# The sums of the FFN input's blocks, made by pairs of token tiles as they leave the norm

## The chip, the cores and the metric

The kernel runs on one core of one Trainium2 chip. The metric is the time of one execution in device microseconds (us); the median of three runs is shown. A core has five engines that each work through a list of instructions in its own order: TensorE (PE, with its weight loads as PEld), VectorE (DVE), ScalarE (ACT), GpSimd (POOL) and SyncE (SP). SP issues nearly all DMAs here. An instruction that waits for a semaphore holds back all that stand behind it on its engine.

## The reference

One inference step of one layer: attention and a diagonal state-space branch, merged and projected by `w_out`, and then a gated feed-forward part (FFN), for 1024 prompt tokens and 64 sample tokens in float32. The part that matters here:

```python
x = x + _rmsnorm(merged @ W['w_out'], W['norm_mix_post'])
f = _rmsnorm(x, W['norm_ffn_pre'])                 # (1088, 1024)
f = (jax.nn.silu(f @ W['w_ffn_gate']) * (f @ W['w_ffn_up'])) @ W['w_ffn_down']   # D_FF = 2816
x = x + _rmsnorm(f, W['norm_ffn_post'])
```

## The kernel before, in words

**Numbers in two halves.** A float32 operand is split into a high part (ACT rounds it to fp32r, line 125) and a low part (DVE takes the difference, line 126). A product then takes three matmuls, high by high, high by low and low by high. `split` is this pair of an ACT and a DVE instruction.

**The mix stage** (`mix_out`). The tokens go through in nine tiles, 8 (the 64 sample tokens), then 0 to 7 of 128 tokens. For a tile, PE makes the product with `w_out` in two banks of 512 columns (lines 137 to 139, 48 matmuls), then `post` normalizes it and adds the residual (ACT line 982, POOL line 148, DVE line 986, POOL line 987), SP writes it to DRAM (`x2`), and `pre` normalizes it once more (ACT line 1010, DVE line 1012), transposes it on PE (line 1016, two groups of four 128 by 128 transposes, each group in one bank of PSUM, tag `tr`, of which there are two) and splits each group into `H`. `H` holds the FFN's input by features: [128, 8 groups of features, high and low, 1088 tokens]. Three tiles' banks let PE run ahead of the norms.

**The FFN's first half** (`ffn_in`). `D_FF` is cut into 11 parts of 256, p = 0 to 10, and each part has a step for the gate weights and one for the up weights. The input is cut into 2 by 2 blocks, features 0 to 511 and 512 to 1023 (r) by tokens 0 to 511 and 512 to 1023 (c). p = 0 (`ffn_first`) is a plain product: for c = 0 gate and up, then for c = 1. Each of p = 1 to 10 uses Winograd's form of Strassen's scheme: seven block products in place of eight, with sums of input blocks (`t1` to `t4`, high and low) on one side and sums of weight blocks (`s1` to `s4`, POOL line 1120, then split) on the other. With X11, X12, X21, X22 for the input's blocks (feature half, token half), the sums are t1 = X12 - X11, t2 = X22 - t1, t3 = X22 - X12 and t4 = X21 - t2. `wino_mm` (line 1184) issues twelve matmuls of 512 columns per block product. The 64 sample tokens go by `decode_rows` (line 1160), whose operand `HD` is a copy of H's last 64 columns (ACT line 1192).

**The token sums** (`wino_tokens`, lines 1056 to 1090). After `ffn_first`, DVE and POOL add the halves in `H` again to whole numbers, make the sums, and split them: t2, t3 and t4 into tiles `T2`, `T3`, `T4`, and t1 over block (0, 1) of `H`, which only p = 0 needs in its plain form. They use buffers (`c`, `s`, `st`) that the weight sums use too.

**The down weights' sums** (`down_sums`). For each p, POOL makes the sums of the down weights' blocks and SP writes them to DRAM (`td`); the second half of the FFN, after p = 10, reads them.

**What sets the order.** The code is recorded in the order of the loops, and a scheduler then orders each engine's instructions by its own model of when each would be ready. The order is fixed when the program is built, for each engine and for SP's queue of DMAs. So a buffer's number of copies (`bufs`) decides who waits for whom, and the scheduler's order decides who stands behind the one that waits.

Of the kernel before, what the change touches and what calls it, by code (L numbers as in the profile page):

```python
# [8 lines left out]
F32 = mybir.dt.float32  # L9
F32R = mybir.dt.float32r  # L10
BF = mybir.dt.bfloat16
AF = mybir.ActivationFunctionType
# [3 lines left out]

D = 1024
SEQ = 1024
# [3 lines left out]
HD = 64  # L22
SBW = 512
FF = 2816
EPS = 1e-6
T = 8
NCH = SEQ // T + 1 + DEC // T
S0 = SEQ // T + 1
CH = ((0, 364), (364, 362), (726, 362))
# [39 lines left out]
class Net:  # L69
# [5 lines left out]
    def consts(self):  # L75
# [22 lines left out]
        nc.vector.memset(self.mhalf, -0.5)  # L98
        self.H = K.tile([128, 8, 2, TOK], F32R, name="H")

# [200 lines left out]
    def ssm_tables(self, P, S):  # L301
# [79 lines left out]
        lp, lpc, fp = pair(lam), pair(lam, True), pair(f)  # L381
        wt = S.tile([128, 2, 16, T, 16], F32, name="wt")
        tm = [S.tile([128, 2, 16, 16], F32, name=f"tm{i}", tag=f"tm{i}") for i in range(2)]
        self.cmul(V, wt[:, :, :, 0], braw, braw[:, ::-1], *bc(fp, 16), tm)
        for n in range(1, T):
            x = wt[:, :, :, n - 1]
# [614 lines left out]
            nc.vector.scalar_tensor_tensor(x[:, s], fg[:, s], rs, xres[:, s], op0=OP.mult, op1=OP.add)  # L1001
            nc.sync.dma_start(out[:, s], x[:, s])

    def pre(self, P, x, gb, hi, lo):

        nc = self.nc
        r = x.shape[0]
        ss = P.tile([128, 4], F32, "ss", "ss")[:r]
        xn = P.tile([128, D], F32, "xn", "xn")[:r]
        nc.scalar.activation(xn, x, AF.Square, scale=1 / 32.0, accum_out=ss[:, 0:1])  # L1010
        rs = self.rstd(P.pool, ss[:, 0:1])
        nc.vector.scalar_tensor_tensor(xn, x, rs, gb[:r], op0=OP.mult, op1=OP.mult)
        for k0 in (0, 4):
            ps = self.ps.tile([128, 512], F32, name="tr", tag="tr")
            for k in range(4):
                nc.tensor.transpose(ps[:, k * 128:k * 128 + r], xn[:, (k0 + k) * 128:(k0 + k + 1) * 128], self.ident[:r, :r])
            self.split(hi[:, k0:k0 + 4], lo[:, k0:k0 + 4], ps.rearrange("p (k t) -> p k t", k=4)[:, :, :r])

    def rows(self, dst, prompt, sample, t):
        self.nc.sync.dma_start(dst, prompt[t * 128:(t + 1) * 128] if t < 8 else sample)  # L1020
# [9 lines left out]
    def mix_out(self, P, U):  # L1030
        nc = self.nc
        self.x2 = self.dram.tile([TOK, D], F32, name="x2")
        gb, gp = self.bcast(P, "norm_mix_post"), self.bcast(P, "norm_ffn_pre")
        for t in (8, 0, 1, 2, 3, 4, 5, 6, 7):
            r, c0 = 128 if t < 8 else DEC, t * 128
            xr = P.tile([128, D], F32, "xr", "xr")[:r]
            self.rows(xr, self.I["x_prompt"][0], self.I["x_sample"][0], t)
            x = P.tile([128, D], F32, "xo", "xo")[:r]
            f = []
            for n in range(2):  # L1040
                s = slice(n * 512, (n + 1) * 512)
                ps = self.ps.tile([128, 512], F32, name="pj", tag="pj")
                if t < 8:
                    self.mm3(ps, [self.hk(k, c0, 128) + (h[:, s], l[:, s]) for k, (h, l) in enumerate(U)])
                    f.append(ps)
                else:
                    self.mm2(ps, [(self.HS[:, k], h[:, s], l[:, s]) for k, (h, l) in enumerate(U)])
                    y = P.tile([128, D], F32, "xn", "xn")[:r, :512]
                    self.low_rows(y, ps, x[:, s])
                    f.append(y)  # L1050
            self.post(P, f, gb, xr, x, x)
            nc.sync.dma_start(self.x2[c0:c0 + r], x)
            self.pre(P, x, gp, *(self.H[:, :, i, c0:c0 + r] for i in range(2)))


    def wino_tokens(self, PT, P):

        nc = self.nc
        V, G = nc.vector, nc.gpsimd
        T = {n: PT.tile([128, 4, 2, 512], F32R, name=f"T{n}") for n in (3, 2, 4)}  # L1060
        H = self.H
        blk = lambda r, c, k: [H[:, 4 * r + k, i, 512 * c:512 * c + 512] for i in range(2)]
        x12 = [P.tile([128, 512], F32, "c", n) for n in ("u11", "u21", "u22", "x")]
        x22 = [P.tile([128, 2, 512], F32, "s", "s")[:, i] for _ in range(2) for i in range(2)]

        def tmp(n):
            return P.tile([128, 512], F32, "st", "st")

        for k in range(4):
            V.tensor_add(x12[k], *blk(0, 1, k))  # L1070
            V.tensor_add(x22[k], *blk(1, 1, k))
            t = tmp("x3")
            V.tensor_sub(t, x22[k], x12[k])
            self.split(T[3][:, k, 0], T[3][:, k, 1], t)
        for k in range(4):
            t = tmp("x11")
            G.tensor_add(t, *blk(0, 0, k))
            V.tensor_sub(x12[k], x12[k], t)
            V.tensor_sub(x22[k], x22[k], x12[k])
            self.split(T[2][:, k, 0], T[2][:, k, 1], x22[k])  # L1080
        for k in range(4):
            self.split(*blk(0, 1, k), x12[k])
        for k in range(4):
            t = tmp("x21")
            G.tensor_add(t, *blk(1, 0, k))
            V.tensor_sub(t, t, x22[k])
            self.split(T[4][:, k, 0], T[4][:, k, 1], t)
        two = lambda t: (t[:, :, 0], t[:, :, 1])
        self.B = dict(b11=self.block(0, 0), b21=self.block(1, 0), b22=self.block(1, 1), t1=self.block(0, 1),
                      t2=two(T[2]), t3=two(T[3]), t4=two(T[4]))  # L1090

    def block(self, r, c):
        return tuple(self.H[:, 4 * r:4 * r + 4, i, 512 * c:512 * c + 512] for i in range(2))
# [34 lines left out]
        h = lambda d, n: tuple(x[:, :, n * 128:(n + 1) * 128] for x in d)  # L1128
        return D, dict(a11=h(D[0], 0), a12=h(D[1], 0), a22=h(D[1], 1), s1=s1, s2=s2, s3=s3, s4=s4)

    def ffn_first(self, P, w, HD):

        nc = self.nc
        D = [self.wino_weights(P, w[up], 0, up, sums=False) for up in range(2)]
        g = {}
        for c in range(2):
            for up in range(2):
                for n in range(2):
                    ps = self.ps.tile([128, 512], F32, name="w", tag=("wx", "wz")[up])
                    for r in range(2):  # L1140
                        self.wino_mm(ps, tuple(x[:, :, n * 128:(n + 1) * 128] for x in D[up][r]), self.block(r, c), start=r == 0, stop=r == 1, whole=True)
                    if not up:
                        x = g[f"{n + 1}{c + 1}"] = P.tile([128, 512], F32, "c", f"g{n + 1}{c + 1}")
                        nc.scalar.activation(x, ps, AF.Silu)
                    else:
                        x = g[f"{n + 1}{c + 1}"]
                        nc.vector.tensor_mul(x, x, ps)
            if not c:
                for up in range(2):
                    Q = self.ps.tile([128, 512], F32, name="wd", tag="wd")[:, :256]  # L1150
                    self.decode_rows(Q, self.decode_pairs(HD, D[up]), 0, 16)
                    self.decode_gate(P, Q, up, 0)
        self.act_sums(0, g, {x: P.tile([128, 512], F32, "c", "u" + x) for x in ("11", "22", "21")})
# [33 lines left out]
    def ffn_in(self, PT, P):  # L1187

        nc = self.nc
        V, A = nc.vector, nc.scalar  # L1190
        HD = P.pool.tile([128, 8, 2 * DEC], F32R, name="HD")
# [3 lines left out]
        self.td = self.dram.tile([11, 4, 128, 512], F32, name="td")  # L1195
        w = [self.I[n][0].rearrange("(k p) n -> p k n", p=128) for n in ("w_ffn_gate", "w_ffn_up")]

        self.ffn_first(P, w, HD)
        self.down_sums(P, 0)
        self.wino_tokens(PT, P)  # L1200
        B = self.B
        for p in range(1, 11):
            for up in range(2):
# [6 lines left out]
                c = {x: P.tile([128, 512], F32, "c", ("u" if up else "g") + x) for x in ("11", "12", "21", "22") if not (up and x == "12")}  # L1210
# [21 lines left out]
                    V.tensor_mul(g[x], g[x], X if x == "12" else c[x])  # L1232
                self.act_sums(p, g, c)
            self.down_sums(P, p)

    def act_sums(self, p, g, c):

# [216 lines left out]
def body(tc, I, O, dbg=None, upto=99):  # L1454
    with ExitStack() as ctx:
        N = Net(ctx, tc, I, O, dbg, upto)
        nc = tc.nc
# [27 lines left out]
        with pool("in", "right") as P0, pool("emb") as PE:  # L1485
            first = todo[:2]
            two = [N.gates(W, m, u) for m, u in zip(first, N.norm_in(P0, PE, first))]
# [50 lines left out]
        with pool("wout", "right") as PW:  # L1538
            N.HS = PW.tile([128, 8, 2 * DEC], F32R, name="HS")
            with pools(tc, "mrgB", dict(braw=1, ga=2, gs=2)) as P:  # L1540
                raw = mA[0].tile([128, TOK], F32, "braw", "braw")
                N.merge(P, Braw, raw)
                U = N.mix_slabs(PW, 0, WO)
            mA[0].__exit__(None, None, None)
            with pools(tc, "mix", dict(ss=4, xo=2, xn=2, xr=2)) as P:
                U += N.mix_slabs(P.pool, WO, 8)
                N.mix_out(P, U)
        with pool("tok", "right") as PT, pools(tc, "ffn1", dict(raw=2, dh=1, dl=1, st=3, s=4, g11=1, g12=1, g21=1, g22=1, u11=1, u21=1,
                                                                  u22=1, q=1, y0=1, y1=1, yo=1, x=1)) as P:
            N.ps.alias = WAL  # L1550
            N.ffn_in(PT, P)
        PA = ctx.enter_context(pools(tc, "acc", dict(ss=4, xr=1, xn=2, hT0=1, hT1=1)))
# [35 lines left out]
```

## Time and profile before

| | us |
|---|---|
| median of 3 runs (lowest to highest) | 1815.24 (1814.98 to 1816.43) |
| the profiled execution | 1819.19 |
| its span, first to last instruction | 1817.4 |
| PE busy | 1704.4 (94%) |
| DVE busy | 1040.1 (57%) |
| ACT busy | 728.3 (40%) |
| POOL busy | 524.9 (29%) |

The profile is of one execution, and all times below are microseconds from the start of its span. A busy PE is not a PE at its peak: a matmul's end is modelled, and matmuls overlap, so the distance between the starts says more than the length of one. The mix stage lies at about 865 to 956, the FFN's first half at 942 to 1454, p = 1 begins at 995.

### The profile page before, as it was taken

The page shows a single profiled execution, that of the slowest core. Times are in us where ns is not written, and L with a number is a line of the kernel's source. Part 1 is how long each engine was busy: PE and PEld are TensorE (multiplying, and loading weights), DVE is VectorE, ACT ScalarE, POOL GpSimd, SP SyncE. Part 2 cuts the span into 40 slices and gives each one's busy share as a digit, 9 for nine tenths or more (in the row PEclk, how much of TensorE's full clock was granted, in tenths as well). Part 3 has the DMA queues.
Part 4 walks back from the last instruction along what each step waited for, and adds up shares of the span by engine and source line. Part 5 has one row for each costly group of instructions (what it writes and reads, how often), then busy time and mean ns, then how long its engine had stood idle before and what let it go on. Part 6 is the DMA issues. An engine that isn't in the chain of part 4 may idle for free.

```text
span 1817.4 us, 24624 instructions
## 1 busy us (share of the span) xinstructions
PE 1704.4 (94%) x9092; PEld 1486.6 (82%) x9092; DVE 1040.1 (57%) x1589; ACT 728.3 (40%) x1349; POOL 524.9 (29%) x454
## 2 busy tenths in 40 slices
PE   8999897999999889999999499999999999979998
PEld 6999897988898878798887388888888888858786
DVE  7438725426767777855443865555555444445465
ACT  6431124125555555633322433333333333443443
POOL 2026000012323232233331654444444200031264
PEclk9999898999999998899999799999999999999999
DMA  8352544684443432157333154444444475665232
GB/s 285 96 137 61 119 99 133 219 223 109 103 106 98 94 101 82 45 182 233 124 102 102 42 174 153 146 140 141 147 142 129 142 252 174 196 197 188 91 104 87
DMA packets 209704, 249.83 MB, mean 137 GB/s; under 512 B 25376, under 2 KB 159632, under 8 KB 209568
## 3 DMA queue, kind: packets, MB, share of 16 engines
q1 hardware_dynamic: 208928, 246.81, 45.0%
q0 software_dynamic: 656, 1.44, 0.6%
q8 instruction: 72, 1.18, 0.3%
q14 instruction: 48, 0.39, 0.1%
HBM read 161.13 MB, written 72.32 MB: 128 GB/s over the span
## 4 chain that ended last, share of the span: by engine, by line
PE 74%; DVE 12%; DMA 5%; ACT 3%; issue 2%; POOL 1%; SPq 1%; DVEq 0%; POOLq 0%; ACTq 0%
PE pj L1184 13%; PE tr L1184 7%; PE pj L137 6%; PE pj L139 6%; PE pj L138 6%; PE pj L1350 3%; PE z L1350 3%; DVE p L730 3%; PE z L1184 3%; PE av L806 2%; PE z L138 2%; PE z L139 2%; PE z L137 2%; PE av L1350 2%; PE tr L1350 2%
## 5 line engine op out<-in xcount | busy, mean ns | idle before, releaser
L137 PE MATMUL pj<-H,wh 128*128 128x362 f32 (+3 forms) x648 | 218.0, 337 | 6.1 <-DVE ql L629 3.4
L139 PE MATMUL pj<-H,wl 128*128 128x362 f32 (+3 forms) x648 | 215.2, 333 | 0.6 <-DVE wl L115 0.6
L138 PE MATMUL pj<-H,wh 128*128 128x362 f32 (+3 forms) x648 | 214.8, 332 | 0.0
L126 DVE TENSOR_TENSOR wl<-raw,wh 128x1024 fp32r<-128x1024 f32 x96 | 129.6, 1352 | 122.5 <-ACT wh L125 122.2
L732 POOL TENSOR_TENSOR w<-w,p 128x383 f32<-128x383 f32 (+4 forms) x68 | 92.6, 1371 | 315.3 <-DVE w L734 187.2
L125 ACT ACTIVATE wh<-raw 128x1024 fp32r<-128x1024 f32 x96 | 101.1, 1057 | 124.5 <-PE z L1350 55.9
L137 PEld LDWEIGHTS pj<-H,wh 128*128 128x128 f32 x648 | 123.0, 190 | 7.8 <-DVE ql L629 3.6
L139 PEld LDWEIGHTS pj<-H,wl 128*128 128x128 f32 x648 | 122.7, 189 | 1.5 <-DVE wl L115 0.8
L138 PEld LDWEIGHTS pj<-H,wh 128*128 128x128 f32 x648 | 122.9, 190 | 1.0 <-issue 0.4
L1184 PE MATMUL pj<-H,s 128*128 128x512 f32 x480 | 118.2, 395 | 0.0
L1184 PEld LDWEIGHTS pj<-H,s 128*128 128x128 f32 x480 | 89.8, 188 | 20.8 <-DVE c L1219 0.3
L125 ACT ACTIVATE s<-st 128x512 fp32r<-128x512 f32 x80 | 50.1, 628 | 125.3 <-PE pj L1184 110.9
L126 DVE TENSOR_TENSOR s<-st,s 128x512 fp32r<-128x512 f32 x80 | 66.0, 827 | 46.9 <-ACT s L125 46.0
L148 POOL TENSOR_TENSOR rs<-rs,mhalf 128x1 f32<-128x1 f32 (+1 forms) x54 | 34.7, 644 | 181.8 <-DVE rs L147 181.5
L119 ACT ACTIVATE wh<-raw 128x1024 fp32r<-128x1024 f32 (+1 forms) x52 | 46.6, 898 | 94.8 <-PE av L138 46.3
L781 DVE TENSOR_TENSOR wtl<-tr,wth 128x512 fp32r<-128x512 f32 (+2 forms) x112 | 55.3, 496 | 50.7 <-ACT wth L780 50.3
L780 ACT ACTIVATE wth<-tr 128x512 fp32r<-128x512 f32 (+2 forms) x112 | 50.3, 453 | 84.6 <-PE tr L776 43.9
L115 DVE TENSOR_TENSOR wl<-raw,wh 128x1024 fp32r<-128x1024 f32 (+1 forms) x50 | 51.1, 1021 | 56.5 <-ACT wh L119 56.5
L1120 POOL TENSOR_TENSOR st<-raw 128x512 f32<-128x512 f32 x40 | 57.6, 1442 | 75.9 <-DVE s L126 41.5
L1184 PE MATMUL tr<-T,s 128*128 128x512 f32 x240 | 62.3, 399 | 17.1 <-ACT s L125 17.1
L728 ACT ACTIVATE p<-z 128x512 f32<-128x512 f32 (+4 forms) x116 | 59.0, 509 | 42.7 <-PE z L830 16.7
L730 DVE TENSOR_TENSOR_SCAN p<-p,zero 128x384 f32<-128x384 f32 (+4 forms) x68 | 73.9, 1094 | 0.2
(558 smaller groups left out, 4672.1 us busy)
## 6 DMA issues: line engine op xcount, KB each, us to landing
sd<-c SPq DMA_DIRECT2D x77, 256.0 KB, 2.7
raw<-sd SPq DMA_DIRECT2D x77, 256.0 KB, 2.8
raw<-in_w_in_dram SPq DMA_DIRECT2D x32, 512.0 KB, 5.4
raw<-in_w_ffn_gate_dram SPq DMA_DIRECT2D x22, 512.0 KB, 3.8
raw<-in_w_ffn_up_dram SPq DMA_DIRECT2D x22, 512.0 KB, 4.7
wd<-in_w_ffn_down_dram SPq DMA_DIRECT2D x44, 256.0 KB, 3.5
td<-wd SPq DMA_DIRECT2D x22, 512.0 KB, 3.2
raw<-td SPq DMA_DIRECT2D x44, 256.0 KB, 3.1
```

The source lines that it names most:

```text
L125: self.nc.scalar.activation(wh, raw, AF.Copy)
L126: self.nc.vector.tensor_sub(wl, raw, wh)
L137: self.nc.tensor.matmul(out, wh, xh, start=i == 0, stop=False)
L138: self.nc.tensor.matmul(out, wh, xl, start=False, stop=False)
L139: self.nc.tensor.matmul(out, wl, xh, start=False, stop=i == n - 1)
L728: nc.scalar.activation(p, z, AF.Sigmoid, scale=-1.0)
L730: nc.vector.tensor_tensor_scan(p[:, ::-1], p[:, ::-1], self.zero.to_broadcast([128, n]), 1.0 if carry is None else carry, op0=OP.mult, op1 ...
L732: (nc.gpsimd if e == 'g' else nc.vector).tensor_tensor(w[:, :n - 1], w[:, :n - 1], p[:, 1:], op=OP.mult)
L781: nc.vector.tensor_sub(wl[:, a:b], ps[:, a:b], wh[:, a:b])
L1120: op(t, x, y)
L1184: self.nc.tensor.matmul(out, a[i][:, k], b[j][:, k], start=start and k == i == j == 0, stop=stop and k == 3 and i == 1, skip_group_check=n ...
L1350: nc.tensor.matmul(B[b + n], x[:, 0, c], y[:, 1], start=new and p == j == 0, stop=p == 10 and j == 2, skip_group_check=not new)
```

## The change

The sums of the input's blocks are no longer made from `H` after p = 0. The tiles now go in the order 8, 0, 4, 1, 5, 2, 6, 3, 7, so that tiles t and t + 4 (the same place in token halves 0 and 1) follow each other. `token_sums` gives two hooks, called by `pre` behind the split of each transposed group: that of tile t copies the group out of PSUM (ACT, line 1030), that of tile t + 4 forms the sums of 128 tokens (DVE), splits them into a tile `ts`, of which there is one, and writes it to a DRAM tensor `tk` (line 1035): four sums for each of four pairs, 16 writes of 512 KB in runs of 512 bytes. `wino_tokens` now only loads T2, T3 and T4 (2 MB each, line 1098), and is recorded in `ffn_first` behind the weights of p = 0; `wino_first` reloads block (0, 1) of `H` with t1 (2 MB, line 1105) after p = 0. `down_sums` of p = 0 moves behind that of p = 5. The mix pool gets four more tiles per partition, the FFN's pool loses one.

```diff
-    def pre(self, P, x, gb, hi, lo):
+    def pre(self, P, x, gb, hi, lo, hook=None):
...
             self.split(hi[:, k0:k0 + 4], lo[:, k0:k0 + 4], ps.rearrange("p (k t) -> p k t", k=4)[:, :, :r])
+            if hook:
+                hook(k0 // 4, ps)
+
+    def token_sums(self, P, t):
+        nc = self.nc
+        V = nc.vector
+        x1 = [None, None]
+
+        def first(r, ps):
+            x1[r] = P.tile([128, 512], F32, "x1", f"x{r}")
+            nc.scalar.activation(x1[r], ps, AF.Copy)
+
+        def put(n, x):
+            s = P.tile([128, 4, 2, 128], F32R, "ts", "ts")
+            self.split(s[:, :, 0], s[:, :, 1], x.rearrange("p (k t) -> p k t", k=4))
+            nc.sync.dma_start(self.tk[n, :, :, :, t * 128:(t + 1) * 128], s.bitcast(F32))
+        y = [None]
+
+        def second(r, ps):
+            if not r:
+                y[0] = P.tile([128, 512], F32, "t1", "t1")
+                V.tensor_sub(y[0], ps, x1[0])
+                put(0, y[0])
+                return
+            t2 = y[0]
+            V.tensor_sub(t2, ps, t2)
+            put(1, t2)
+            V.tensor_sub(x1[0], t2, x1[0])
+            put(2, x1[0])
+            V.tensor_sub(x1[1], x1[1], t2)
+            put(3, x1[1])
+        return first, second
...
+        self.tk = self.dram.tile([4, 128, 4, 2, 512], F32, name="tk")
-        for t in (8, 0, 1, 2, 3, 4, 5, 6, 7):
+        hooks = {}
+        for t in (8, 0, 4, 1, 5, 2, 6, 3, 7):
+            if t < 4:
+                hooks[t], hooks[t + 4] = self.token_sums(P, t)
...
-            self.pre(P, x, gp, *(self.H[:, :, i, c0:c0 + r] for i in range(2)))
+            self.pre(P, x, gp, *(self.H[:, :, i, c0:c0 + r] for i in range(2)), hook=hooks.get(t))
...
-        for k in range(4):
-            V.tensor_add(x12[k], *blk(0, 1, k))
-            V.tensor_add(x22[k], *blk(1, 1, k))
-            t = tmp("x3")
-            V.tensor_sub(t, x22[k], x12[k])
-            self.split(T[3][:, k, 0], T[3][:, k, 1], t)
...
+    def wino_tokens(self, PT):
+        T = [PT.tile([128, 4, 2, 512], F32R, name=f"T{n}") for n in (2, 3, 4)]
+        for i in (1, 0, 2):
+            self.nc.sync.dma_start(T[i].bitcast(F32), self.tk[i + 1])
...
+    def wino_first(self):
+
+        self.nc.sync.dma_start(self.H[:, 0:4, :, 512:SEQ].bitcast(F32), self.tk[0])
...
-        self.ffn_first(P, w, HD)
-        self.down_sums(P, 0)
-        self.wino_tokens(PT, P)
+        self.ffn_first(P, w, HD, PT)
+        self.wino_first()
...
             self.down_sums(P, p)
+            if p == 5:
+                self.down_sums(P, 0)
...
-            with pools(tc, "mix", dict(ss=4, xo=2, xn=2, xr=2)) as P:
+            with pools(tc, "mix", dict(ss=4, xo=2, xn=2, xr=2, x0=1, x1=1, t1=1, ts=1)) as P:
```

The first place where the scheduler's order matters is ACT, from the last tile's splits into `H` to the first up weights. Before:

```order
L125 ACTIVATE H<-tr 128x4x128 [waits PE_49] x2
L1192 ACTIVATE HD<-H 128x1024
L1144 ACT_TABLE_LOAD [waits DMAHW3_49]
L1144 ACTIVATE c<-pj 128x512 [waits Activation_49]
L1144 ACTIVATE c<-pj 128x512
L125 ACTIVATE wh<-raw 128x1024 [waits DMAHW5_49]
```

The same place in the changed kernel, where `ts<-t` and `ts<-x` are the ACT halves of the splits of the last pair's four sums, `x_9364<-tr` is the copy of tile 3, and a wait for a semaphore named DMAHW is one for a DMA:

```order
L125 ACTIVATE H<-tr 128x4x128 [waits PE_49]
L1030 ACTIVATE x_9364<-tr 128x512 [waits DVE_49]
L125 ACTIVATE H<-tr 128x4x128 [waits PE_49]
L125 ACTIVATE ts<-t_9443 128x4x128 [waits DMAHW0_49,DVE_49]
L125 ACTIVATE ts<-t_9443 128x4x128 [waits DMAHW1_49,DVE_49,Activation_49]
L125 ACTIVATE ts<-x_9355 128x4x128 [waits DMAHW2_49,DVE_49]
L125 ACTIVATE ts<-x_9364 128x4x128 [waits DMAHW4_49,DVE_49]
L1208 ACTIVATE HD<-H 128x1024
L1160 ACT_TABLE_LOAD
L1160 ACTIVATE c<-pj 128x512 x2
L125 ACTIVATE wh<-raw 128x1024 [waits DMAHW7_49]
L125 ACTIVATE wh<-raw 128x1024 [waits DMAHW0_49]
```

Four splits into the one tile `ts`, each behind a DMA, now stand between the last split into `H` and the copy `HD`. The second place is SP's queue from the last write of `x2` to the weights of p = 0's up step. Before:

```order
L1052 DMA x_8619<-xo 128x1024 [waits DMAHW3_49,Pool_49]
L1052 DMA x_8619<-xo 128x1024 [waits Pool_49]
L1102 DMA raw<-in_w_ffn_up_dram 128x4x256 [waits DMAHW5_49,PE_49]
L1102 DMA raw<-in_w_ffn_up_dram 128x4x256 [waits PE_49]
L1254 DMA wd<-in_w_ffn_down_dram 128x2x256 [waits DMAHW7_49,DMAHW5_49,DVE_49]
```

In the changed kernel, behind its last write of `x2`, with T_9508 to T_9510 for T2 to T4:

```order
L1035 DMA tk<-ts 1024x1x128 [waits DMAHW1_49,DVE_49]
L1035 DMA tk<-ts 1024x1x128 [waits DMAHW2_49,DVE_49]
L1098 DMA T_9508<-tk 128x4096 [waits DMAHW3_49,DMAHW6_49,DMAHW2_49,PE_49]
L1035 DMA tk<-ts 1024x1x128 [waits DMAHW4_49,DVE_49]
L1098 DMA T_9509<-tk 128x4096 [waits DMAHW5_49,DMAHW7_49,DMAHW4_49,PE_49]
L1035 DMA tk<-ts 1024x1x128 [waits DVE_49]
L1117 DMA raw<-in_w_ffn_up_dram 128x4x256 [waits PE_49]
L1117 DMA raw<-in_w_ffn_up_dram 128x4x256 [waits DMAHW0_49,PE_49]
L1098 DMA T_9510<-tk 128x4096 [waits DMAHW6_49,DMAHW1_49]
```

The up weights of p = 0 stood directly behind the last `x2`; they now stand behind the writes of the pieces and behind T2 and T3, which wait for those writes.

## Rows read from the trace of the kernel before

**Rows 1.** The page, TensorE's busy tenths in 40 slices of 45.4 us.
```profile
PE   8999897999999889999999499999999999979998
```

**Rows 2.** Windows: stretch, us; busy us (count) per engine; PEclk, DMA share, GB/s.
```profile
963.50:994.80 31.30, 31.30 (x144) 25.50 (x143) 7.42 (x11) 4.93 (x7) 5.74 (x8) 1.00 0.37 119
994.80:1044.50 49.70, 25.51 (x120) 20.87 (x119) 43.58 (x54) 18.44 (x31) 27.94 (x16) 0.76 0.17 55
1086.60:1429.40 342.80, 342.80 (x1606) 282.79 (x1605) 195.48 (x232) 124.77 (x208) 149.64 (x131) 1.00 0.45 143
```

**Rows 3.** Timeline of PE, 1009 to 1046: start, us, ..., [idle before <-releaser].
```profile
1016.93 0.45 PE L1175 MATMUL av<-ident,y 64*128 64x64 f32 x2 [7.07 <-DVE y L1172]
1034.50 4.66 PE L1184 MATMUL tr<-T,s 128*128 128x512 f32 x12 [17.12 <-ACT s L125]
1039.00 2.90 PE L1184 MATMUL pj<-T,s 128*128 128x512 f32 x12
```

**Rows 4.** Chain of waits, 860 to 1110: start, us, what.
```profile
...
1007.39 2.28 POOL st L1077
...
1031.52 1.75 DVE st L1086
1033.83 0.62 ACT s L125
...
```

**Rows 5.** Groups by form, 865 to 956: count, then busy us, mean ns.
```profile
L126 DVE TENSOR_TENSOR H<-tr,H 128x512 fp32r<-128x512 f32 x15 | 9.9, 685 | 5.5 <-ACT H L125 5.5
L125 ACT ACTIVATE H<-tr 128x512 fp32r<-128x512 f32 x16 | 8.9, 594 | 13.8 <-PE tr L1016 13.8
```

**Rows 6.** Timeline of PE, 920 to 945, two tiles' transposes.
```profile
921.27 1.03 PE L1016 MATMUL tr<-ident,xn 128*128 128x128 f32 x8
932.14 1.03 PE L1016 MATMUL tr<-ident,xn 128*128 128x128 f32 x8
```

**Rows 7.** DMA issues: count, KB each, median us from issue to landing.
```profile
...
raw<-sd SPq DMA_DIRECT2D x77, 256.0 KB, 2.8
raw<-in_w_in_dram SPq DMA_DIRECT2D x32, 512.0 KB, 5.4
raw<-in_w_ffn_up_dram SPq DMA_DIRECT2D x22, 512.0 KB, 4.7
td<-wd SPq DMA_DIRECT2D x22, 512.0 KB, 3.2
x<-xo SPq DMA_DIRECT2D x8, 512.0 KB, 2.9
ad<-o SPq DMA_DIRECT2D x11, 64.0 KB, 1.6
...
```

**Rows 8.** Timeline of PE, 942 to 965.
```profile
942.54 0.64 PE L1184 MATMUL pj<-H,wh 128*128 128x512 f32 x2
...
957.11 0.39 PE L1160 MATMUL z<-wh,HD 128*128 128x256 f32 x1 [1.68 <-ACT HD L1192]
...
963.46 1.10 PE L1184 MATMUL tr<-H,wh 128*128 128x512 f32 x4
```

**Rows 9.** Timeline of ACT, 941 to 964.
```profile
955.99 1.06 ACT L1192 ACTIVATE HD<-H 128x1024 fp32r<-128x1024 f32 x1
```

**Rows 10.** Timeline of DVE, 943 to 946.
```profile
945.01 0.74 DVE L986 SCALAR_TENSOR_TENSOR xo<-z,rs,gb_norm_mix_post 128x512 f32<-128x512 f32 x1
```

**Rows 11.** Windows, a stretch at the kernel's start; last two columns DMA share, GB/s.
```profile
21.50:26.50 5.00, 2.40 (x17) 1.93 (x15) 4.42 (x6) 4.44 (x9) 3.28 (x3) 1.00 1.03 417
```

**Rows 12.** Timeline of SP, 843 to 848.
```profile
844.39 0.38 SPq L950 DMA_DIRECT2D gb_norm_ffn_pre<-in_norm_ffn_pre_dram  x1
844.82 0.68 SPq L1020 DMA_DIRECT2D xr<-in_x_sample_dram  x1
```

**Rows 13.** DMA issues between 843.4 and 846: count, KB, us to landing.
```profile
...
gb_norm_ffn_pre<-in_norm_ffn_pre_dram SPq DMA_DIRECT2D x1, 512.0 KB, 7.6
...
xr<-in_x_sample_dram SPq DMA_DIRECT2D x1, 256.0 KB, 8.6
```

More of the change, by code (lines that the diff above doesn't have):

```diff
@@ L1052, in mix_out @@
             nc.sync.dma_start(self.x2[c0:c0 + r], x)
-            self.pre(P, x, gp, *(self.H[:, :, i, c0:c0 + r] for i in range(2)))
[L1056 to L1067, printed above, removed]
-        for k in range(4):
-            V.tensor_add(x12[k], *blk(0, 1, k))
-            V.tensor_add(x22[k], *blk(1, 1, k))
-            t = tmp("x3")
-            V.tensor_sub(t, x22[k], x12[k])
-            self.split(T[3][:, k, 0], T[3][:, k, 1], t)
[L1075 to L1087, printed above, removed]
+            self.pre(P, x, gp, *(self.H[:, :, i, c0:c0 + r] for i in range(2)), hook=hooks.get(t))
[3 more added lines that the diff above has]
+            self.nc.sync.dma_start(T[i].bitcast(F32), self.tk[i + 1])
         two = lambda t: (t[:, :, 0], t[:, :, 1])
         self.B = dict(b11=self.block(0, 0), b21=self.block(1, 0), b22=self.block(1, 1), t1=self.block(0, 1),
-                      t2=two(T[2]), t3=two(T[3]), t4=two(T[4]))
+                      t2=two(T[0]), t3=two(T[1]), t4=two(T[2]))
+    def wino_first(self):
+        self.nc.sync.dma_start(self.H[:, 0:4, :, 512:SEQ].bitcast(F32), self.tk[0])
     def block(self, r, c):
@@ L1129, in wino_weights, with ffn_first @@
         return D, dict(a11=h(D[0], 0), a12=h(D[1], 0), a22=h(D[1], 1), s1=s1, s2=s2, s3=s3, s4=s4)
-    def ffn_first(self, P, w, HD):
+    def ffn_first(self, P, w, HD, PT):
         nc = self.nc
         D = [self.wino_weights(P, w[up], 0, up, sums=False) for up in range(2)]
+        self.wino_tokens(PT)
         g = {}
@@ L1548, in body @@
         with pool("tok", "right") as PT, pools(tc, "ffn1", dict(raw=2, dh=1, dl=1, st=3, s=4, g11=1, g12=1, g21=1, g22=1, u11=1, u21=1,
-                                                                  u22=1, q=1, y0=1, y1=1, yo=1, x=1)) as P:
+                                                                  u22=1, q=1, y0=1, y1=1, yo=1)) as P:
             N.ps.alias = WAL
```

## The prediction

> **What bounds the kernel now.** I read the page first: TensorE's line of slices is nearly all eights and nines, and its one slice at 4, the 23rd, stands in the FFN [rows 1]. The windows by stage come next. Their busy times stand in the order PE, PEld, DVE, ACT, POOL. From 963.5 to 994.8 PE never idles; from 994.8 to 1044.5 it is busy 25.51 of 49.70 us, while DVE is busy 43.58; from 1086.6 to 1429.4 it never idles again [rows 2]. So this change touches the one hole that PE has in the FFN. The timeline of PE gives its size: idle 7.07 us before 1016.93 and 17.12 us before 1034.50, together 24.2, the same as 49.70 - 25.51. The twelve matmuls after it take 4.66 us and the next twelve 2.90, at a granted clock that the windows put at 0.76 for the whole stretch, so between its two levels of 1.2 and 2.4 GHz; 4.66 - 2.90 or 1.8 us more are lost there [rows 2, 3]. The chain of waits names what ends the hole: the DVE and POOL steps of the token sums (lines 1070 to 1086), one after the other, then the first split weight sum [rows 4]. The removed stall is worth 24.2 + 1.8 = **26.0 us**.
>
> **What the change removes.** 24 elementwise DVE sums, 8 POOL sums and 16 splits leave the stretch 957 to 1034, and POOL is free there for the weight sums of p = 1 (line 1120), which now wait until 1031. If nothing took their place, PE would pass from p = 0 to p = 1 without a gap. The eight POOL steps and six DMAs of the down weights for p = 0 go from before p = 1 to after p = 5; POOL is busy 150 of 343 us in that part [rows 2] while PE never waits, so I cost that at nothing; uncovered it would be a few us of POOL.
>
> **What it adds, and where.** Per pair of token tiles ACT gets 2 copies and 4 splits, DVE 4 sums and 4 splits, at 0.6 and 0.7 us each [rows 5]: 3.6 and 5.5 us against the 22 us that PE needs for a pair (transposes 10.9 us apart, 921.27 and 932.14, where PE sets the pace [rows 6]). Throughput hides that. What it doesn't hide is a queue of one: all sixteen pieces go through one buffer `ts`, so the ACT half of a split waits until the DMA of the piece before has landed, and everything behind it on ACT waits too. The order on ACT has, after the last H split, four such splits, and only then the copy `HD` (line 1192 before, 1208 now), Silu's table, the two Silus and the splits of the up weights. The order on SP has the loads T2 and T3 between the last writes, and the up weights of p = 0 behind all of them.
>
> The price of one piece: ACT split 0.6, DVE split 0.7 [rows 5], about 0.1 for the handovers, and the write. No row has that write (512 KB in runs of 512 B). From below: x<-xo, the same bytes in longer runs, lands in 2.9; from above: raw<-in_w_in, the same bytes in the same runs but read from an input, lands in 5.4. Nearest is td<-wd, same bytes and direction, runs of 1 KB, 3.2 [rows 7]. I take 3.4, so a piece takes **4.8 us**, four pieces 19.2: under PE's 22, so the earlier pairs keep up, but the pairs of tiles 2 and 6 and of 3 and 7 come at the end back to back.
>
> The chain then, in the times of this execution:
> - PE's last w_out matmul ends where line 1184 begins now, 942.5 [rows 8]. Tile 6's second half is transposed only behind it. ACT then has three splits (1.8), DVE the two steps of line 986 that end at 945.75 [rows 10] and two splits (1.4); the first piece of tiles 2 and 6 is issued at about 947.0.
> - Five pieces on, 971.0, the sixth is issued; it lands at 974.4. That releases T2 (2 MB) on SP. A stretch in which reads are queued up moves 417 GB/s [rows 11], so T2's data takes 5.0, and with the 2.2 that a read needs beyond its data (raw<-sd, 256 KB, lands in 2.8 [rows 7], of which 0.6 is data at that rate) it lands at 981.6. At td<-wd's data rate (512 KB in 3.2 less the 1.6 of the small write ad<-o [rows 7]) T2 and T3 would take 6.4 each; that end is kept for the range.
> - The seventh piece is issued at 975.8 behind T2. Requests are served in order: a read of 256 KB, issued 0.4 us behind one of 512 KB that takes 7.6, takes 8.6 [rows 12, 13]. It lands 1.8 after T2 (3.4 less ad<-o's 1.6): 983.4.
> - The eighth split and HD (0.6 + 1.06 [rows 9]) end at 985.1: the decode matmuls, at 957.1 now, start there, and all of PE's order stands behind them.
> - T3 goes out at 983.4 and lands at 990.6, the eighth piece 1.8 later, the first up weights 1.6 after that (512 KB in runs of 1 KB, as td<-wd less ad<-o [rows 7]): 994.0. With ACT's 1.06 for a tile of that size [rows 9], PE's first matmul on them starts at 995.1 instead of 963.46 [rows 8]: **31.6 us late**. What lies between (decode, 12 matmuls, the late transposes of tiles 3 and 7) hides in this wait. So does the slow clock after it: its 4.7 us [rows 3] end before 995.
>
> From there to p = 1 PE has 31.3 us of unbroken work [rows 2], as before. In p = 1 I see no new wait: T2 and T3 have landed, T4 lands near 999, and the reload of H (2 MB, about 7.2 us, issued at PE's last read of that block, some 3 us before p = 1) is needed only after 48 matmuls and 8 decode rows (12 us). Sum: 31.6 - 26.0 = **+5.6 us**. The profiled execution took 1819.19 (a span of 1817.4 and 1.8 around it), so it would be 1824.8; the median of the runs shown is 3.95 lower, 1815.24, which gives 1820.8.
>
> **A rule against the row.** The row has 417 GB/s for a backlog of reads. The Trainium skill ("DMA: Bandwidth & Descriptors", Specifications) gives a limit of about 358 GB/s of HBM per core; with that T2 and T3 would take 5.9 each by an estimate from that page, and the time would be 1822.6. The trace is above that limit in those 5 us, so I keep its number.
>
> **Rivals.**
> - *The transfers overlap, and the puts are cheap* (faster). If a later, smaller write needn't wait for T2 and T3, the seventh piece lands at 979.2, the eighth is issued at 980.6, the up weights right behind it land after their own 4.7 [rows 7], and PE starts at 987.1: 23.6 - 26.0, 1812.8. With x<-xo's 2.9 per write, six writes save 3 more: 1809.8. It decides where PE's first up matmul starts before 985.9 (963.5 + 26.0 - 3.6). The reads that queue up at 844 speak against it [rows 12, 13]. The Trainium skill ("DMA: Bandwidth & Descriptors", Queues, rings and completion order) says that a later descriptor may finish its write before an earlier one; by that rule this rival is open, but the 8.6 us of the small read don't show it.
> - *The writes in short runs are slow.* At raw<-in_w_in's 5.4 a piece takes 6.8, a pair 27, more than PE's 22, so the pieces fall behind from the first pair. The six steps up to T2 cost 12 more, the two pieces behind T2 and T3 two each: 1837.
> - *The change does what it says and nothing takes its place*: 26.0 saved, 1789. It needs HD and the up weights not to stand behind the pieces; the orders on ACT and SP say that they do.
> - *H comes back late.* If SP reaches its reload only behind the gate weights of p = 2, whose buffer is freed by POOL, the margin of some 8 us goes, and each us beyond it is one of PE's; with 5 of them 1826.
>
> **How the numbers follow.** Forecast 0.61, overlap 0.14, slow writes 0.15, nothing in its place 0.05, late H 0.05. The measurement tells 0.2%, 3.6 us, from no change. The forecast's own range runs from +2 (2.9 per write, eight times 0.5 less) to +13 (T2 and T3 at 6.4, and 4.0 per write): 1817 to 1828, of which I give 0.20 to within 0.2% and 0.41 to slower. The overlap gives 0.10 faster and 0.04 same; the full gain 0.05 faster; the last two 0.20 slower. Together 0.15, 0.24 and 0.61, and I move 0.02 from slower to faster and 0.01 to same for what I have not thought of. The range reaches to the cheap overlap below and to slow writes above: 1809 to 1836.
>
> **What would show it.** Right: PE's hole before line 1184's `tr<-T,s` is gone, and there are two new ones, one of 15 to 25 us before the decode matmuls, ended by ACT's HD, one of 2 to 8 us before the up matmuls, ended by the up weights; ACT waits for DMA before the splits into `ts`; tk<-ts lands in about 3.4, but the one behind T2 in 7 or more; p = 1 starts near 1026 and has no gap. Wrong: HD within a few us of 960; tk<-ts at 2.5 or at 5 and more; the write behind T2 no later than the others; a wait of PE in p = 1 for H or for a weight sum.

## The result, and the profile after

| | before | after |
|---|---|---|
| median of 4 runs (lowest to highest), us | 1815.11 (1810.88 to 1816.43) | 1832.05 (1829.75 to 1833.75) |
| the profiled execution, us | 1819.19 | 1833.31 |
| its span, us | 1817.4 | 1831.5 |

The changed kernel is slower: the ratio is 1.0097, with an interval of 1.0075 to 1.0118, or some 17 us. The forecast was 1820.8, within 1809 to 1836: the direction and the mechanism came as forecast, but the time is 11 us more, and it lies above the likeliest case's own range (1817 to 1828).

TensorE's slices on the page of the changed kernel, the line that answers to [rows 1]. The hole is as deep as before or deeper, a 3 in the 22nd slice where the 23rd had a 4:

```profile
PE   8999797999999989899993999999999999979998
```

The waits of TensorE from 900 to 1100: operation and line, what ended the wait, us in total, times, longest.

```profile
PE z L1176 <- ACT HD L1208: 23.6, 1, 23.6
PE tr L1200 <- ACT wh L125: 4.9, 1, 4.9
PE tr L1016 <- ACT x L1030: 4.4, 2, 2.2
```

The old hole before `tr<-T,s` [rows 3] is gone, and the two new ones stand where the prediction put them, 15 to 25 us before the decode matmuls and 2 to 8 before the up matmuls. The third, for the copies that the hooks make (line 1030 holds the bank of the transposes), was not forecast. The chain of waits of the same execution, from 905 on (start, us, what):

```profile
909.25 3.49 DMA tk<-ts
...
914.70 3.51 DMA tk<-ts
...
936.38 3.48 DMA tk<-ts
...
948.33 3.50 DMA tk<-ts
951.94 0.64 ACT ts L125
952.61 0.70 DVE ts L126
953.33 3.46 DMA tk<-ts
...
972.98 3.46 DMA tk<-ts
...
977.90 8.43 DMA tk<-ts
986.41 0.64 ACT ts L125
...
988.35 10.95 DMA raw<-in_w_ffn_up_dram
999.33 1.06 ACT wh L125
```

Where before the token sums stood in this chain [rows 4], it now goes from piece to piece: write 3.5, ACT 0.64, DVE 0.70, next write. The pieces are in it from 909 on, two pairs earlier than the prediction had them. SP's queue shows who stands in front of the up weights (start, us to issue, line, tiles, count):

```profile
976.50 0.33 SPq L1098 DMA_DIRECT2D T<-tk  x1
977.90 0.51 SPq L1035 DMA_DIRECT2D tk<-ts  x1
986.39 0.33 SPq L1098 DMA_DIRECT2D T<-tk  x1
987.79 0.51 SPq L1035 DMA_DIRECT2D tk<-ts  x1
988.35 5.13 SPq L1117 DMA_DIRECT2D raw<-in_w_ffn_up_dram  x2
```

And windows, with the columns of [rows 2]: the stretch of the first wait, the restart behind the second, the rest of p = 0, from p = 1 to the up step of p = 2, and the undisturbed part.

```profile
943.90:988.00 44.10, 16.62 (x60) 12.22 (x60) 17.16 (x24) 10.02 (x16) 2.91 (x2) 0.67 0.50 150
...
1000.44:1006.40 5.96, 5.96 (x15) 4.70 (x16) 4.79 (x5) 2.90 (x5) 3.73 (x3) 0.50 0.95 380
1006.40:1035.80 29.40, 29.40 (x136) 23.97 (x135) 6.58 (x8) 4.94 (x8) 1.46 (x2) 1.00 0.20 60
1035.80:1100.00 64.20, 64.20 (x303) 53.17 (x302) 36.08 (x43) 23.68 (x39) 30.52 (x27) 1.00 0.52 178
1100.00:1444.10 344.10, 344.10 (x1618) 284.09 (x1617) 194.18 (x231) 124.77 (x207) 155.89 (x137) 1.00 0.46 149
```

The up matmuls start at 1000.44 and run at 0.50, the lower level of 1.2 GHz, until about 1006; p = 1 starts at 1035.8 and has no gap.

**A measure for the runs that follow.** Single executions differ by a few us before the mix stage. So for each run I also give the distance from PE's first `w_out` matmul to the first matmul with a weight sum in p = 2's up step, which holds all that the change touches but the move of `down_sums(0)`. In the changed kernel these two are the rows

```profile
834.53 0.40 PE L968 MATMUL z<-t,HS 128*128 128x512 f32 x1
...
1100.02 0.86 PE L1200 MATMUL tr<-T,s 128*128 128x512 f32 x3
```

so 265.5 us; before they are 836.01 and 1086.6, 250.6 us (the profile has eleven of the twelve matmuls there, from 1086.83 on, and I count one back at 0.23; so in e1 and e11 too). I call it **the section**. It accounts for 14.9 of the some 17 us.

### The profile page after: what moved, and what is told of

It is laid out like the page before. It is cut to its first block, busy times and chain, and to the rows that moved or that the text cites. A ratio compares the mean times of both kernels' runs of the same rounds, so it can differ in the third digit from the quotient of the medians.

```text
span 1831.5 us, 24687 instructions
## 1 busy us (share of the span) xinstructions
PE 1705.9 (93%) x9092; PEld 1485.7 (81%) x9092; DVE 1031.4 (56%) x1581; ACT 732.1 (40%) x1357; POOL 513.0 (28%) x446
## 4 chain that ended last, share of the span: by engine, by line
PE 65%; DVE 13%; DMA 12%; ACT 4%; issue 3%; POOL 2%; SPq 1%; DVEq 0%; POOLq 0%; ACTq 0%
PE pj L1200 13%; PE tr L1200 7%; PE pj L137 5%; PE pj L139 5%; PE pj L138 5%; PE z L1367 3%; PE pj L1367 3%; DVE p L730 3%; PE z L1200 3%; DMA tk<-ts 3%; PE av L1367 2%; PE tr L1367 2%; PE av L806 1%; PE tr L776 1%; DMA gd<-gl 1%
## 5 line engine op out<-in xcount | busy, mean ns | idle before, releaser
L1200 PE MATMUL pj<-H,wh 128*128 128x512 f32 x224 | 74.7, 408 | 2.4 <-ACT H L125 1.4
L728 ACT ACTIVATE p<-z 128x512 f32<-128x512 f32 (+4 forms) x116 | 59.0, 509 | 42.7 <-PE z L830 16.7
```

What stands on the lines that cost most here:

```text
L728: nc.scalar.activation(p, z, AF.Sigmoid, scale=-1.0)
L1200: self.nc.tensor.matmul(out, a[i][:, k], b[j][:, k], start=start and k == i == j == 0, stop=stop and k == 3 and i == 1, skip_group_check=n ...
```

## The experiments

Each was timed over several rounds beside the kernel before, on the same chip; a ratio is to the kernel before, with its 95% interval.

| run | median, us | ratio | section, us |
|---|---|---|---|
| before | 1814.3 to 1815.9 in its series | 1 | 250.6 |
| after | 1832.05 | 1.0097 [1.0075, 1.0118] | 265.5 |
| e1_order | 1817.25 | 1.0014 [1.0005, 1.0023] | 250.8 |
| e2_two_ts | 1813.15 | 0.9993 [0.9984, 1.0001] | 248.8 |
| e3_up_first | 1818.77 | 1.0022 [1.0010, 1.0033] | 253.0 |
| e4_hd_early | 1830.97 | 1.0087 [1.0074, 1.0101] | 264.6 |
| e5_ts_hd_up | 1803.42 | 0.9937 [0.9925, 0.9949] | 239.9 |
| e6_up_pool | 1803.59 | 0.9937 [0.9924, 0.9950] | some 237 |
| e7_warm | 1830.88 | 1.0086 [1.0074, 1.0098] | 265.8 |
| e8_long_runs | 1822.73 | 1.0048 [1.0036, 1.0059] | 258.7 |
| e9_all_long | 1802.91 | 0.9927 [0.9915, 0.9940] | 235.1 |
| e10_pool_split | 1803.33 | 0.9931 [0.9919, 0.9942] | 237.6 |
| e11_down_sums | 1814.60 | 0.9996 [0.9985, 1.0006] | 249.8 |
| e12_one_xr | 1830.83 | 1.0089 [1.0075, 1.0102] | 265.5 |

**The theory**: the stall was traded for a queue of one through `ts`, and for loads that stand ahead of the up weights. **Rivals**: the tile order itself, the short runs of the writes, the wait for HD as such, the lower clock.

**e1, the tile order alone**, in the kernel before:

```diff
-        for t in (8, 0, 1, 2, 3, 4, 5, 6, 7):
+        for t in (8, 0, 4, 1, 5, 2, 6, 3, 7):
```

> The kernel before with the tile order 8, 0, 4, 1, 5, 2, 6, 3, 7 alone; the sums are still made from H after p = 0. Theory (the loss comes from the pieces and the loads, not from the order): PE's gate matmuls of p = 0 now need tile 3, the last but one, so they start some 1 to 2 us later than 942.5, of which the 1.68 us that PE waited for HD anyway takes most; +0.5 us, from 0 to 2: 1815.6. Rival (the order itself delays the FFN): PE waits for tile 3's splits before the gate matmuls, 5 us or more, at the lower clock behind it: 1822.

The section stays, 250.8 against 250.6, so the order costs nothing where the change acts, and the rival falls. The time rose by 2.5 us, more than the 0 to 2 expected. In the profiled executions they lie behind the FFN's first half: from its last matmul to the end it takes 365.8 us against 363.5. The scheduler also ordered a few matmuls of the second half otherwise; that these are the cause isn't shown. In the changed kernel that tail is 362.9, so this is no part of its loss.

**e2, two tiles `ts`**, with one `xr` in place of two for the room, **and e12, one `xr` alone**:

```diff
-            with pools(tc, "mix", dict(ss=4, xo=2, xn=2, xr=2, x0=1, x1=1, t1=1, ts=1)) as P:
+            with pools(tc, "mix", dict(ss=4, xo=2, xn=2, xr=1, x0=1, x1=1, t1=1, ts=2)) as P:   # e2
+            with pools(tc, "mix", dict(ss=4, xo=2, xn=2, xr=1, x0=1, x1=1, t1=1, ts=1)) as P:   # e12
```

> The changed kernel with two tiles ts in place of one; for the room, one tile xr in place of two (the rows of x, loaded ahead). Theory (a queue of one): two writes are under way at once, so the pieces follow each other every (1.4 + 3.5) / 2 = 2.45 us in place of 4.92; the sixth piece of the last eight is issued near 960.6 in place of 972.98, HD ends near 966 in place of 988.0. The up weights still stand behind T2 and T3: up matmuls near 986.5 in place of 1000.4, so 14 us less than the changed kernel: 1818. Rival (the writes share one limit, so that two take twice as long): the pieces keep 4.9 and nothing changes: 1832.

> The changed kernel with one tile xr in place of two and one ts: the other half of the edit of the run with two tiles ts. Theory (a load of 512 KB per 10.9 us needs no second tile): 1832, within 2. Rival (the load comes late for POOL's residual sum): some us slower, 1836; if it is faster, the gain of the run with two tiles is not all that of ts.

e12 is the changed kernel again, 265.5; so what e2 gains, 19 us in the medians and 16.7 in the section, belongs to the second `ts`. The chain of waits of e2:

```profile
963.75 3.46 DMA tk<-ts
967.29 0.63 ACT ts L125
967.92 0.95 ACT HD L1208
...
972.92 12.23 DMA raw<-in_w_ffn_up_dram
985.18 1.06 ACT wh L125
986.29 2.07 PE tr L1200 x4
```

The last four pieces are issued at 961.10, 963.75, 966.03 and 968.68, so 2.5 us apart in place of 4.92; the writes overlap by some 1 us, and the first two still take 3.5, the third 4.1, the fourth, behind T2, 10.0. HD ends at 968.9 in place of 988.0, and the up matmuls start at 986.3, where 986.5 was expected. That agreement is in part luck: in this execution the mix stage began 2.95 us earlier, so that 11.2 of the 14 us are its own. PE's wait for the copies of line 1030 is gone as well. What is left is the load of the up weights, 12.2 us behind T2 and T3.

**e3, the loads of T2 to T4 behind the up weights** in SP's queue, one `ts`:

```diff
-            nc.sync.dma_start(x, w[:, 4 * r:4 * r + 4, p * 256:(p + 1) * 256])
+            self.lastw = nc.sync.dma_start(x, w[:, 4 * r:4 * r + 4, p * 256:(p + 1) * 256])
...
-        self.wino_tokens(PT)
+        with self.tc.issue_after(self.lastw.ins):
+            self.wino_tokens(PT)
```

The last load that `lastw` names there is that of the up weights' second half.

> The changed kernel with the loads of T2, T3 and T4 held behind the up weights of p = 0 in SP's queue; ts stays one tile. Theory (two terms, chain of pieces and loads ahead of the weights): the pieces keep 4.92 but the seventh and eighth no longer wait behind T2 and T3: eighth piece issued near 982.8, HD ends near 983.3, up weights issued near 983 and landed near 988, up matmuls near 989 in place of 1000.4, 11 us less: 1821. Rival (T2 and T3 are late then, and p = 1 waits for them): T2 lands after 1003, still before p = 1 at 1024, so this would show as a wait of PE in p = 1 and give back up to 11: 1832.

The chain of waits, a window of the ten us in which T3, T2 and T4 were queued up together, and one from the start of the up matmuls:

```profile
975.26 3.49 DMA tk<-ts
...
980.82 5.86 DMA raw<-in_w_ffn_up_dram
```

```profile
984.00:994.00 10.00, 9.75 (x41) 7.48 (x40) 5.14 (x5) 3.97 (x6) 6.19 (x4) 0.96 1.04 409
987.80:994.00 6.20, 6.05 (x25) 4.74 (x26) 5.13 (x5) 2.91 (x5) 3.97 (x3) 1.00 1.01 428
```

The pieces keep their 4.92, but the up matmuls start at 987.8, 12.6 us sooner, of which 2.6 only because this mix stage began earlier, and p = 1 waits for nothing. 13 us of the loss go (12.5 in the section), 11 were expected: the loads ahead of the weights are the second term. The other 2.4 us of the section lie behind the start of the up matmuls. PE doesn't wait for them here, they run at a clock of 1.00, and from them to p = 1 the same matmuls take 32.9 us, where they take 35.3 in the changed kernel, whose first 6 us run at 0.50. So 2.4 us is what the lower clock cost there.

**e4, HD copied early**, by a place in the pool of T2 to T4:

```diff
-        HD = P.pool.tile([128, 8, 2 * DEC], F32R, name="HD")
+        HD = PT.tile([128, 8, 2 * DEC], F32R, name="HD")
```

> The changed kernel with HD in another pool, so that its copy stands on ACT ahead of the last pair's pieces; nothing else. Theory (HD is not what binds, the up weights are): PE's 23.6 us wait for HD goes, and the wait for the up weights grows from 4.9 to some 27; up matmuls at 999.4 to 1000.4: 1831.5. Rival (the wait for HD that the trace shows is the cost): the 23.6 us come back, 1808.

PE's waits from 900 to 1100:

```profile
PE pj L1200 <- ACT c L1160: 24.7, 1, 24.7
...
PE tr L1200 <- ACT wh L125: 2.4, 1, 2.4
```

The longest wait of the trace, 23.6 us for HD, was taken away, and the time stayed (1830.97): the wait came back 24.7 long in front of the next instruction, for Silu, which stands on ACT behind the same four pieces. A wait's length in a profile is not its price.

**e5, the three together** (two `ts`, T2 to T4 behind the up weights, HD early), **and e6**, where the up weights go through POOL's queue in place of the order on SP:

```diff
-            nc.sync.dma_start(x, w[:, 4 * r:4 * r + 4, p * 256:(p + 1) * 256])
+            self.lastw = (nc.sync if sums or not i else nc.gpsimd).dma_start(x, w[:, 4 * r:4 * r + 4, p * 256:(p + 1) * 256])
```

> The edits of the three runs before together: two tiles ts (one xr), T2 to T4 behind the up weights, HD copied early. Theory (three terms that add): the sixth piece of the last eight is issued near 964, as with two tiles alone; the eighth near 968.5, the up weights right behind it, landing 5.9 later near 975; up matmuls near 976 in place of 986.3 with two tiles alone and 1000.4 in the changed kernel: 1803. Rival (the two gains overlap, since with two tiles the up weights are late only by T2 and T3's data, which has to move anyway before p = 1): p = 1 waits for T3 or T2 and the sum stays near 1812.

> As the run before, but the up weights of p = 0 are loaded through POOL's queue, which passes its last sum of the mix stage near 945, and T2 to T4 need no place behind them. Theory: the weights lie ready, and ACT's last four pieces alone set the start: the eighth piece's split near 968, Silu's table and Silus behind it, up matmuls near 972.5, 3.5 less than the run before: 1799.5. Rival (POOL's queue is slow, or its transfer competes with the writes): up weights after 976, 1805 or more.

e5 beats both kernels, at 1803.42 where 1803 was expected: the terms add for the most part. Apart they gave back 33 us (30 in the section), together 29 (26). Its one wait of size, and the chain that ends it:

```profile
PE pj L1201 <- ACT c L1161: 11.7, 1, 11.7
```

```profile
962.23 3.46 DMA tk<-ts
965.77 0.63 ACT ts L125
966.42 1.28 ACT L1161
967.71 0.61 ACT c L1161
968.36 7.51 PE pj L1201 x25
```

e6 had its weights ready and gained nothing over e5 in time (1803.59, where 1799.5 was expected): the same 11.7 us, for Silu behind the last pieces, and in e5 PE no longer waited for the weights. Its section can't be set beside that of e5: five of the twelve matmuls that end it ran 10 us ahead of the others there, and I counted them back.

**e7, matmuls in the waits**, to keep PE busy:

```diff
+                    for _ in range(110 if not up else 0):
+                        nc.tensor.matmul(Q, D[0][0][0][:, 0, :128], self.block(0, 0)[0][:, 0], start=True, stop=True)
...
+                    for _ in range(20 if up and not c and not n else 0):
+                        nc.tensor.matmul(ps, D[0][0][0][:, 0, :128], self.block(0, 0)[0][:, 0], start=True, stop=True)
```

> The changed kernel with 110 more matmuls of 512 columns into the bank of the decode rows before these, and 20 into the up step's first bank before its own; they fill PE's two waits and their results are overwritten. Theory (4.0 us of the loss is the lower clock behind the waits): at 0.21 us each, 23 us, they end before HD at 988; up matmuls still start at 1000.4, but from there to p = 1 it takes 31.4 us in place of 35.4, and the time falls by 4: 1828. Rival (the 4.0 us are not the clock but waits for weights of p = 1): unchanged, 1832; if they run at the lower clock throughout, they end near 1000 and the time rises.

The 20 further ones were meant for the wait before the up matmuls; the scheduler placed them ahead of the decode matmuls too, so the long wait was filled and two short ones, 3.0 and 4.5 us, stayed. The windows:

```profile
944.00:984.00 40.00, 40.00 (x183) 32.92 (x181) 14.38 (x20) 7.72 (x13) 2.49 (x2) 1.00 0.50 157
987.20:990.50 3.30, 3.30 (x17) 3.30 (x18) 0.00 (x0) 2.34 (x3) 0.00 (x0) 0.56 0.83 338
998.63:1004.20 5.57, 5.57 (x14) 4.41 (x15) 4.77 (x5) 2.90 (x5) 3.34 (x3) 0.50 0.94 373
```

PE was busy without a break at full clock for 40 us, and still ran at 0.56 and 0.50 behind the short waits. From the up matmuls to p = 1 it took 35.3 us, as in the changed kernel (35.3); the section is the same, 265.8. My expectation failed twice: the clock was not kept, and 4.0 us were too much to lay on it. Counting starts in the changed kernel's trace, 14 matmuls follow each other at 0.43 us where 0.23 is the pace at full clock, 2.7 us in all, close to the 2.4 by which e3 is shorter there; the other 1.3 us are about five matmuls that before ran ahead of the up step and now behind its start. Whether a filled wait gives the clock back wasn't shown.

**e8, long runs**: `tk` and T2 to T4 laid out by token tiles, so that a piece is written in runs of 4 KB.

```diff
-            nc.sync.dma_start(self.tk[n, :, :, :, t * 128:(t + 1) * 128], s.bitcast(F32))
+            nc.sync.dma_start(self.tk[n, :, t], s.bitcast(F32).rearrange("p k i c -> p (k i c)"))
...
```

> The changed kernel with tk, T2, T3 and T4 laid out by token tiles, so that a piece is written in runs of 4 KB in place of 512 B; the reload of H goes in four DMAs. Theory (the run length is a small part of a piece): tk<-ts lands in 2.9, as x<-xo before, in place of 3.5; six pieces bring the up weights 3.6 us earlier, 1828.5. Rival 1 (the short runs are what makes the pieces slow): below 2 us a write, 1823 or less. Rival 2 (they cost nothing): 3.5 and 1832.

The chain of waits, and behind it the row of the first of the last eight pieces:

```profile
959.53 2.59 DMA tk<-ts
...
963.61 2.60 DMA tk<-ts
...
967.67 8.82 DMA tk<-ts
...
978.32 10.73 DMA raw<-in_w_ffn_up_dram
```

```profile
942.67 0.32 SPq L1035 DMA_DIRECT2D tk<-ts  x1
```

A write lands in 2.60 in place of 3.46, so a piece takes 4.07. The time fell by 9 us and the section by 6.8, where 3.6 were expected: a write is 0.86 shorter and not 0.6, and the last eight pieces aren't all. Counted from the first `w_out` matmul (830.95 here, 834.53 in the changed kernel), the first of the last eight is issued 111.7 us in, where it was 113.8, and the seventh 136.7 us in, where it was 143.4. So 2.1 of these 6.7 us were lost ahead of the last eight, in the pieces of the first two pairs. The write behind T2 and the weights behind T3 take about as long as before, 8.8 and 10.7. The short runs are thus part of the price, with one `ts`.

**e9, e5 with e8's layout, and e10**, with POOL's queue for the up weights (e6) and POOL's arithmetic for the last pair's last two pieces:

```diff
...
+            if t < 3 or n < 2:
+                self.split(s[:, :, 0], s[:, :, 1], x)
+            else:
+                self.hi_pool(s[:, :, 0], x)
+                nc.gpsimd.tensor_sub(s[:, :, 1], x, s[:, :, 0])
...
```

> The run with two tiles ts, HD early and T2 to T4 behind the up weights, and tk, T2, T3, T4 laid out by token tiles as well (writes in runs of 4 KB, which landed in 2.6 in place of 3.5). Theory (what is left is a wait for the last pair's pieces, of which two wait for a write): two times 0.9 less there, and the earlier pairs lag less, so that the gate matmuls start up to 4 us sooner, as with the long runs alone (938.2 against 943.9): 1799. Rival (with two tiles the writes no longer set the pace): 1803.4 as without.

> As the run before, with the up weights of p = 0 loaded through POOL's queue (T2 to T4 free again), and the last pair's third and fourth pieces split by POOL in place of ACT and DVE. Theory (PE's 11.7 us wait for Silu is ACT standing behind the last pieces): Silu then waits only for the second piece's write, near 964 in place of 967.7, and the up weights lie ready, so PE has no second wait: 3 us less than the run before, 1796. Rival (POOL's two steps of 1.3 per piece and T2 to T4 behind them are late for p = 1): a wait of PE for T2 or T3, 1800 or more.

e9 has the shortest section, 235.1 against 239.9 in e5, but by their ratios the two can't be told apart, so the layout's worth beside two `ts` stays open. e10 did half of what it should, and none of it shows in the time (1803.33, where 1796 was expected): the wait for Silu fell from 10.9 to 6.3 us, but the up weights were late, with a wait of 3.1 us. POOL issued their loads behind its splits, when SP had already issued T2 and T3, and the first took 14.57 us to land, as POOL's timeline and the chain of waits show:

```profile
964.83 0.62 POOL L122 TENSOR_SCALAR ts<-x 128x512 fp32r<-128x512 f32 x1 [0.58 <-issue]
965.53 1.27 POOL L1039 TENSOR_TENSOR ts<-x,ts 128x512 fp32r<-128x512 f32 x1
966.75 1.63 POOL L1123 DMA_DIRECT2D raw<-in_w_ffn_up_dram  x2
```

```profile
967.62 14.57 DMA raw<-in_w_ffn_up_dram
```

**e11, the move of `down_sums(0)` alone**, in the kernel before:

```diff
-        self.down_sums(P, 0)
         self.wino_tokens(PT, P)
...
             self.down_sums(P, p)
+            if p == 5:
+                self.down_sums(P, 0)
```

> The kernel before with only the down weights' sums of p = 0 moved behind those of p = 5. Theory (they lie beside other work at either place): no difference, 1814.3, within 2. Rival (in the hole before p = 1 POOL is part of the chain of token sums, and its eight steps stand ahead of the weight sums there): up to 5 faster, 1809.

No difference, in the time or in the section (249.8).

## Why the prediction was right, and where it was off

- *The stall that goes*, 26.0 us: from p = 1's start to p = 2's up step it is 64.2 us (1035.8 to 1100.0), where it was 91.8 (994.8 to 1086.6). 27.6, right, 1.6 too low.
- *The price of a piece*, 4.8 us, of it 3.4 for the write: 4.92 and 3.46. The value taken a little above the nearest row, td<-wd [rows 7], was good.
- *"The earlier pairs keep up"* failed. 19.2 against 22 us left 2.8 us per pair, but the pieces of a pair can't be spread over its 22 us: three of the four need its last transposes. The chain of waits runs through `tk<-ts` from 909, PE waits 4.4 us for the copies, and e8 gets back 2.1 us from shorter writes ahead of the last eight pieces. In the times it shows little, by luck: the first of the last eight was issued at 948.33, forecast 947.0, but the profiled mix stage began 1.5 us earlier than before. Counted from the first `w_out` matmul it came 2.8 us later than forecast.
- *Six pieces, T2, the seventh piece, HD*: 971.0, 981.6, 983.4 and 985.1 were forecast; 972.98, 984.8 (976.50 and 8.29), 986.33 and 988.0 came. HD's lateness as a mechanism stands, but e4 shows that it wasn't the bound: the up weights were, 5 us later.
- *T3 and the up weights behind it* was the largest error in a transfer: T3 took 9.94 us, not 7.2, and the up weights landed at 999.3, not 994.0. The up matmuls started at 1000.44, 37.0 late in place of 31.6. Of these 5.4 us 2.1 were there when T2 was issued, 1.1 came in T2 and 2.7 in T3; the steps between them took 0.5 less. e3 shows the mechanism, the weights' place in the queue; the size came from the rate of a queue that is filled with reads. The 417 GB/s [rows 11] are confirmed for a queue of reads, 409 over ten us in e3. But T2 and T3 went out one at a time, each with a write beside it. What makes them slower stays open. It isn't the short runs, since in e8 the write behind T2 took 8.8 as well, and it isn't the write alone: T4, with only reads beside it, took 7.9, where 7.2 was forecast for such a load.
- *The rule weighed against the row*: the Trainium skill ("DMA: Bandwidth & Descriptors", Specifications) has 358 GB/s as the limit, by which T2 needs 5.9 us for its data, an estimate from that page. Its 8.29 less the 2.2 of the prediction is 6.1, nearer to that than to 5.0. Yet e3's 409 shows that such a limit did not bind here; the page "Perfetto Trace Analysis" (Roofline) of the Trainium skill says that a core alone can pull more than that share, and with that the trace agrees.
- *"So does the slow clock after it ... hides in this wait"* failed. The prediction let the lower clock end before 995, behind the decode matmuls; the second wait, of 4.9 us, brought it back, and the up matmuls ran at 0.50. That cost 2.7 us (2.4 by e3), and the matmuls that had moved behind 1.3 more; the prediction had both at nothing.
- *p = 1 without a new wait*, and *`down_sums` at nothing*: both right (the last window of after, e11).
- *The rivals.* "The transfers overlap" fell: the write behind T2 took 8.43 us, as the row of the small read had said. "Slow writes" fell: 3.46, not 5.4. "H late" fell: it landed at 1041.7 and PE didn't wait. "Nothing takes its place" fell with PE's two new waits. (The 987.1 of the first rival is 0.7 more than its own terms give, 980.6 + 4.7 + 1.06.)

In the profiled execution the sum reads 37.0 + 2.7 + 1.3 - 27.6 = 13.4 us, in place of 31.6 - 26.0 = 5.6; the spans differ by 14.1. The mis-sized terms are what stands in front of the up weights (5.4) and the clock behind the last wait with the matmuls that moved (4.0); the stall was 1.6 more, the other way. The remaining 3 us between the spans and the medians are within what single executions differ by. So the mechanism was right, and the loss was three times the forecast. That the time still lies within 1809 to 1836 is in part luck: the upper end was set by slow writes, which did not come.

## What to carry to other kernels

When a sum is moved from engines to a trip through DRAM, its price can be set by the number of buffers it goes through and by what stands behind it in each engine's order and in the DMA queue, not by its arithmetic: here a second buffer of 4 KB a partition gave back 17 to 19 us, the order of five loads 13, and both with an early copy turned a kernel that was 17 us slower into one that is 11 us faster. Look for the next wait behind the one that the profile names, since removing the longest one alone changed nothing. Compare single profiles from a common event and not by their clock times: of e3's 12.6 us 2.6 were only an earlier start. And ask of each pair of steps that must "keep up" not only whether its work fits, but when its last input comes.

## What the runs showed of the hardware that I had not expected

- A write of 512 KB to DRAM landed in 3.46 us in runs of 512 B and in 2.60 in runs of 4 KB (e8); two that overlapped by 0.8 us still took 3.5 each (e2).
- In e7 PE was busy for 40 us without a break at a granted clock of 1.00, waited 3.0 us and then ran at 0.56 for 3.3 us; behind its next wait, of 4.5 us, it ran at 0.50, the level of 1.2 GHz, for 5.6 us.
- A queue that was filled with reads moved 409 GB/s over ten us (e3), but a 2 MB read with a 512 KB write issued 1.4 us behind it took 8.3 to 9.9 us (the changed kernel, T2 and T3). SP itself needed 5.13 us to issue the next two loads of 512 KB, where one T load just before took 0.33.
